# A list scheduler's keys, its model of a shared port, and the order of late loads in a single-core block kernel

## The chip, the cores and the metric

The kernel runs on one core of one Trainium2 chip. The metric is the device time of one execution in microseconds (us), taken as the median of several runs. Five instruction streams work beside each other: TensorE (PE; its weight loads, PEld, overlap its matmuls), VectorE (DVE), ScalarE (ACT), GpSimd (POOL) and SyncE (SP), which here only issues DMAs. Each stream runs its own list in order; between streams there are semaphores.

## The reference

One transformer block on 512 positions of width 1024, in float32: a hybrid attention (8 heads of "NSA": compressed, selected and window keys, gated; 8 heads of a sliding window of 128 with sinks), its output projection, a feed-forward part with a causal convolution (inner width 2816), and a gate from per-layer inputs.

```python
h = rmsnorm(x, attn_pre_g)
q_n, kc, vc, ksl, vsl, kwn, vwn, g_n, q_s, k_s, v_s = split(h @ w_in)
k_cmp, v_cmp = compress_kv(kc), compress_kv(vc)      # gelu(blocks @ w1) @ w2
o_nsa = nsa_attention(q_n, k_cmp, v_cmp, ksl, vsl, kwn, vwn, sigmoid(g_n))
o_swa = swa_attention(q_s, k_s, v_s, sinks)
x = x + rmsnorm(concat([o_nsa, o_swa]) @ w_o, attn_post_g)
a, u = split(rmsnorm(x, mlp_pre_g) @ w_gate_up)
y = (gelu(causal_dwconv(a)) * u) @ w_down
x = x + rmsnorm(y, mlp_post_g)
x = x + (p @ w_ple) * sigmoid(x @ w_ple_gate)
```

## The kernel before

**Arithmetic.** Each float32 operand of a product is split into a high part (a copy in TensorE's rounded format fp32r, mostly made by ACT) and a low part (operand minus high part, a "low pass", one two-operand pass of DVE or POOL). A product is three matmuls: high by high, low by high, high by low. Activations lie with features on the 128 partitions and the 512 positions along the free axis.

**Stages.** `load_x` (L632) loads x in eight chunks together with the weights wv, makes their parts and the sums of squares for the first norm. `v_natural` (L676) makes all values and the gates; `compress_in` (L744), `proj_k`, `proj_q` and `compress_out` (L814) make compressed keys and values, keys and queries. The first heads' scores start near 75 us. The attention runs over 16 units (a group of four heads by a block of 128 queries); between its steps PE gets "fill" products: the remaining key and query projections and the first part of the output projection. `out_proj` finishes the projection, adds up mo (the mixed rows) on DVE, sums their squares with `square_acc` (L558), and issues the loads of p, wple (the "e" product), the residual x and the first gate-up weights gu0 to gu3. Then comes the handover: `norm_add` (L1221) with the reciprocal root of the sums (`rstd_col`, L528: product r_pst on PE, r_rv on DVE, r2c on POOL), the eight products of `ple_tile` around it, and the MLP (mlpup, mlpdown) and the gate behind.

**What sets the order.** From `load_x` to the end of `out_proj` nothing is emitted directly. `Recorder` (L216) keeps each instruction as a `Node` (L165) with the nodes it depends on; tiles get their buffers only when the order is fixed. `schedule` (L280) is a list scheduler: it holds a clock for each stream, a duration for each instruction (`cost`, L245, times MARGIN), 0.2 us or so of lag between engines, the buffers and PSUM banks that are free, and a rate of the DMA wire. At each step it takes the engine whose next instruction could start first, and on it, of those that could start then, the one with the least key. The key is the earliest number, in written order, among the instruction and those that follow from it. `play` (L373) emits the result. The trace shows all these instructions under one line, L376 (L419 in the changed file). What is written behind `out_proj` keeps its written order, and shows as L197.

**Names.** In the trace a row reads output<-input by tile names: `loadx_u` the parts of x, `vnatural_pss` the banks of `v_natural`, `compress_psmm` that of compress's first product, `projk_wh` the parts of the key weights, `nsa_pss` scores, `nsa_nmp`/`nsa_nnm` maxima and sums of a softmax, `fill_wh` weights of fill products, `swa_u` 545 and 548 and `outproj_wr` 652 and 655 the raw gu0 to gu3, `outproj_wh` 649 to 657 their low parts, `outproj_s_605` the sum of squares.

Of the kernel before, what the change touches and what calls it, by code (L numbers as in the profile page):

```python
# [17 lines left out]
P = 128  # L18
T = 512
D = 1024  # L20
KC = D // P
# [52 lines left out]
MARGIN = 1.06  # L74
# [90 lines left out]
class Node:  # L165
    ins = None

    def __init__(self, n, engine, name, a, k):
# [4 lines left out]
        self.writes = [x for m, x in named if m in ("out", "accum_out")] + ([] if "out" in k else views[:1])  # L173
        if "out" not in k and not isinstance(a[0], View):
            self.writes = [x for m, x in named if m == "accum_out"]
# [40 lines left out]
class Recorder:  # L216
    ENGINES = dict(tensor="PE", scalar="ACT", vector="DVE", gpsimd="POOL", sync="SP")

    def __init__(self, nc, pools):
        self.pools, self.nodes, self.on, self.over = pools, [], False, False  # L220
        for e in self.ENGINES:
            setattr(self, e, Engine(self, e, getattr(nc, e)))

    def add(self, engine, name, a, k):
# [15 lines left out]
        for t in node.tiles:  # L240
            t.left += 1
# [3 lines left out]
    def cost(node):  # L245
# [5 lines left out]
        if e == "PE":  # L251
# [4 lines left out]
            return max(.058, .008 + .00043 * n)  # L256
        if e == "ACT":
            t = (.07 if psum else .1) + .00083 * n
            return t + (.17 if "accum_out" in node.k else .02)
        if e == "DVE":  # L260
            if name == "tensor_tensor_reduce":
                return .09 + .00103 * n + (.06 if not isinstance(node.k.get("scalar"), float) and n < 288 else 0)
            if name in ("tensor_copy", "tensor_scalar") and not psum:
                return .07 + .0006 * n
            if name == "memset":
                return .06 + .0007 * n
            if o.shape[0] < P and n >= 256:
                return .2 + .00104 * n
            return .07 + .00106 * n + (.06 if name == "scalar_tensor_tensor" else 0)
        if e == "POOL":  # L270
            if name in ("tensor_tensor",):
                return 1.05
            if name in ("tensor_sub", "tensor_mul", "tensor_add"):
                return .12 + .0023 * n
            if name == "tensor_scalar":
                return .33 + .00085 * n
            return .1 + .0009 * n
        return .05

    def schedule(self, live, begin):  # L280

        nodes = self.nodes
        lag = dict(PE=.25, ACT=.2, DVE=.2, POOL=.25, SP=.1)
        clock = dict(begin)
        for x in nodes:
            x.wait = len(x.deps)
            for d in x.deps:
                d.after.append(x)
        keep = {id(v.tile) for v in live}
        order, spare, have = {}, {}, {}  # L290
        seen = set()
        for x in nodes:
            for t in x.tiles:
                if id(t) not in seen:
                    seen.add(id(t))
                    spare.setdefault(t.key, [-99.0] * t.bufs)
                    if t.tile is not None:
                        spare[t.key].pop()
                    else:
# [1777 lines left out]
```

## Time and profile before

| what | value |
|---|---|
| median of 3 runs | 650.56 us (648.75 to 651.54) |
| the profiled execution | 652.84 us |
| its span in the profile | 651.1 us |
| granted TensorE clock, mean of the span | 0.996 |
| DVE, ACT and POOL busy | 511.8, 396.9 and 165.6 us |
| DMA moved | 95.78 MB, 147 GB/s in the mean |

The span is the profiler's time from the first to the last instruction of one execution. "Busy" counts an engine's instructions, so a pipelined matmul that waits a little still counts as busy. An idle time is put down to the semaphore that came last.

The stages lie in the trace as follows: loads and values until 30 us, first projections until 75, attention until 236, handover until 256, gate-up until 470, then down projection and gate. The page's slices show the granted clock at full speed except in the slice that holds 244 to 260:

```
PE   8999999999999999999999999999999999999997
PEclk9999999999999998999999999999999999999999
```

### The profile page before, as it was taken

Reading aid. Unit: us, or ns where it says so; the run is one execution under the profiler, and the core shown is the slowest. Engines: PE = TensorE matmul, PEld = TensorE weight load, DVE = VectorE, ACT = ScalarE, POOL = GpSimd, SP = SyncE. Lnnn points to the kernel's source line nnn. Section 1 sums busy time; section 2 is a strip of 40 time slices with the busy share of each in tenths; the row PEclk is TensorE's granted clock in tenths of the full one; section 3 lists DMA queues with packets and bytes.
Section 4 is the critical chain, followed back from the end, with each engine's and each line's share of the span. In section 5 each row is a group of like instructions: output and inputs, shape, how many; then the busy total and the mean of one; then the engine's idle time right before and its main releaser. Section 6 shows DMA issues by size and latency. Waiting matters only on the chain.

```text
span 651.1 us, 11311 instructions
## 1 busy us (share of the span) xinstructions
PE 640.6 (98%) x4071; PEld 578.2 (89%) x4071; DVE 511.8 (79%) x1023; ACT 396.9 (61%) x759; POOL 165.6 (25%) x246
## 2 busy tenths in 40 slices
PE   8999999999999999999999999999999999999997
PEld 7978778788888887888999999999998999999986
DVE  7596468788866675799899898998999985756873
ACT  7535477888889655666576767677764443333351
POOL 1010368876858350120101010011100010201000
PEclk9999999999999998999999999999999999999999
DMA  8416643210341637277465756758854334367032
GB/s 300 167 68 175 183 113 98 50 33 17 82 146 66 244 127 290 98 229 176 114 163 178 178 164 144 206 159 240 206 149 145 117 112 123 115 251 262 5 114 81
DMA packets 45289, 95.78 MB, mean 147 GB/s; under 512 B 4401, under 2 KB 13745, under 8 KB 44977
## 3 DMA queue, kind: packets, MB, share of 16 engines
q1 hardware_dynamic: 40208, 84.49, 39.3%
q0 software_dynamic: 4880, 10.49, 9.4%
q8 instruction: 32, 0.52, 0.3%
q14 instruction: 25, 0.20, 0.1%
q10 hardware_dynamic: 144, 0.08, 0.1%
HBM read 81.41 MB, written 9.44 MB: 140 GB/s over the span
## 4 chain that ended last, share of the span: by engine, by line
PE 91%; DVE 4%; ACT 2%; DMA 1%; issue 1%; DVEq 0%; SPq 0%
PE mlpup_psmm L197 23%; PE fill_psmm L376 8%; PE mlpup_pss L197 8%; PE mlpdown_pst L197 6%; PE mlpup_pst L197 5%; PE mlpdown_pss L197 5%; PE mlpdown_psmm L197 4%; PE norm_pss L197 3%; PE nsa_pso L376 3%; PE projq_psmm L376 3%; PE nsa_pst L376 3%; PE nsa_pss L376 2%; PE vnatural_pss L376 2%; PE mlpup_pso L197 2%; PE projk_psmm L376 2%; PE swa_pso L376 1%
## 5 line engine op out<-in xcount | busy, mean ns | idle before, releaser
L197 PE MATMUL mlpup_psmm<-r_u,mlpup_wh 128*128 128x256 f32 (+1 forms) x612 | 79.5, 283 | 0.1
L197 PEld LDWEIGHTS mlpup_psmm<-r_u,mlpup_wh 128*128 128x128 f32 x612 | 76.1, 191 | 0.6 <-DVE mlpup_wh L197 0.4
L197 PE MATMUL mlpup_psmm<-mlpup_u,mlpup_wh 128*128 128x256 f32 (+1 forms) x474 | 69.4, 297 | 0.0
L197 PEld LDWEIGHTS mlpup_psmm<-mlpup_u,mlpup_wh 128*128 128x128 f32 x474 | 63.5, 190 | 2.6
L197 POOL DMA_DIRECT2D mlpup_u<-in_gs_dram x17 | 20.9, 1230 | 155.8 <-DMA mlpup_u<-in_gs_dram 41.2
L197 ACT ACTIVATE mlpup_wh<-mlpup_u 128x1024 fp32r<-128x1024 f32 x37 | 39.2, 1060 | 25.6 <-PE mlpup_psmm L197 21.5
L197 ACT ACTIVATE mlpdown_wh<-mlpdown_wr 128x1024 fp32r<-128x1024 f32 (+1 forms) x24 | 23.7, 988 | 40.3 <-PE mlpdown_pst L197 10.9
L197 DVE TENSOR_TENSOR mlpup_wh<-mlpup_u,mlpup_wh 128x1024 fp32r<-128x1024 f32 x37 | 45.2, 1220 | 1.5 <-ACT mlpup_wh L197 0.5
L376 PE MATMUL fill_psmm<-loadx_u,fill_wh 128*128 128x512 f32 x144 | 45.1, 403 | 0.0
L197 PE MATMUL mlpdown_pst<-mlpup_u,mlpdown_wh 128*128 128x512 f32 (+1 forms) x228 | 44.9, 340 | 0.0
L376 POOL TENSOR_SCALAR nsa_u<-nsa_u,nsa_nrc,gate 128x512 f32<-128x512 f32 (+3 forms) x64 | 38.5, 612 | 12.4 <-DVE nsa_nrc L376 10.1
L197 PEld LDWEIGHTS mlpdown_pst<-mlpup_u,mlpdown_wh 128*128 128x128 f32 x228 | 37.0, 189 | 4.9
L197 DVE TENSOR_TENSOR mlpdown_wh<-mlpdown_wr,mlpdown_wh 128x1024 fp32r<-128x1024 f32 (+1 forms) x24 | 27.2, 1135 | 17.7 <-ACT mlpdown_wh L197 17.6
L376 ACT ACTIVATE nsa_u<-nsa_u,nsa_nnm 128x512 f32<-128x512 f32 (+3 forms) x64 | 35.3, 555 | 5.9 <-DVE nsa_nnm L376 4.6
L197 DVE TENSOR_TENSOR mlpup_wh<-mlpup_wr,mlpup_wh 128x1024 fp32r<-128x1024 f32 (+1 forms) x23 | 27.9, 1212 | 11.8 <-ACT mlpup_wh L197 11.8
L197 POOL TENSOR_TENSOR mlpdown_s<-mlpdown_s,mlpdown_s 128x512 f32<-128x512 f32 x6 | 9.5, 1578 | 106.3 <-ACT mlpdown_s L197 106.1
L197 PE MATMUL mlpdown_pss<-mlpup_u,mlpdown_wh 128*128 128x256 f32 x246 | 35.8, 282 | 0.0
L376 POOL TENSOR_TENSOR fill_wh<-fill_wr,fill_wh 128x1024 fp32r<-128x1024 f32 (+2 forms) x13 | 24.5, 1889 | 33.9 <-DVE compress_u L376 22.2
L197 PEld LDWEIGHTS mlpdown_pss<-mlpup_u,mlpdown_wh 128*128 128x128 f32 x246 | 32.5, 191 | 0.3
L376 DVE TENSOR_TENSOR nsa_u<-nsa_pst,nsa_u 128x512 fp32r<-128x512 f32 (+1 forms) x43 | 28.6, 685 | 4.5 <-ACT nsa_u L376 4.0
L376 DVE CUSTOM_DVE_ANT_0 nsa_u<-nsa_pss,biastables_u 128x128 f32<-128x128 f32 (+4 forms) x64 | 27.3, 446 | 5.0 <-PE nsa_pss L376 2.8
L197 PE MATMUL mlpdown_psmm<-mlpup_u,mlpdown_wh 128*128 128x256 f32 (+1 forms) x180 | 31.1, 320 | 0.0
(342 smaller groups left out, 1669.1 us busy)
## 6 DMA issues: line engine op xcount, KB each, us to landing
mlpup_u<-in_gs_dram SPq DMA_DIRECT2D x34, 512.0 KB, 5.0
mlpup_u<-in_gs_dram POOLq DMA_DIRECT2D x17, 512.0 KB, 6.2
mlpup_wr<-in_gs_dram SPq DMA_DIRECT2D x17, 256.0 KB, 3.9
fill_wr<-in_win_dram SPq DMA_DIRECT2D x6, 512.0 KB, 3.7
fill_u<-fill_u SPq DMA_DIRECT2D x20, 128.0 KB, 2.4
mlpdown_wr<-in_down_dram SPq DMA_DIRECT2D x5, 512.0 KB, 3.7
loadx_u<-in_xT_dram SPq DMA_DIRECT2D x8, 256.0 KB, 5.1
compress_u<-projk_u SPq DMA_DIRECT2D x16, 128.0 KB, 2.4
```

Of the source, the lines that this page charges most:

```text
L197: return f(*map(real, a), **{m: real(x) for m, x in k.items()})
L376: hold(x.call(*map(real, x.a), **{m: real(v) for m, v in x.k.items()}))
```

## The change

Five things are changed.

1. **Keys.** Before, an instruction's key came from written order alone. Now `play` plans six times. After each plan `dues` walks back through it: PE's instructions get the times at which PE would run them without any gap, every other instruction the latest time at which it may start so that whoever follows (also through a buffer that it frees) is in time, and these become the keys of the next plan. What the later stages want is given as time after PE's last recorded instruction: the e product's parts at 0, the sums of squares at 1.2, its second weights at 2.5, mo and x at 4.0, gu at 7.0. The plan with the earliest end is emitted.
2. **A shared port.** In the plan POOL's instructions, and DVE's passes over operands that lie in SBUF (those in SHARED that read no PSUM), exclude each other.
3. **Written order in `load_x`.** There ACT and DVE keep the order as written.
4. **Numbers.** Some durations, MARGIN, and the DMA rate (300 GB/s for 240) change; buffers that come free are told apart.
5. **Two edits of the program.** All sums of squares of `out_proj` are added on DVE (before: on POOL, but for the last). The dummy Exp that makes ACT load its table reads gv, the output of the second Gelu, where it read a constant.

```diff
-MARGIN = 1.06
+MARGIN = 1.1
+PASSES = 6
+SHARED = ("tensor_sub", "tensor_add", "tensor_mul", "scalar_tensor_tensor", "tensor_copy")
...
+        if self.strict and node.engine in ("ACT", "DVE"):
+            if node.engine in self.before:
+                node.deps.add(self.before[node.engine])
+            self.before[node.engine] = node
...
+    def link(self):
...
+            x.port = x.engine == "POOL" or x.engine == "DVE" and x.name in SHARED and not any(v.tile.psum for v in x.reads)
+            x.key = x.n if x.engine != "SP" else min([y.n for y in x.after] or [x.n])
+
+    def dues(self, done, begin, live):
+
+        t = begin["PE"]
+        for x in done:
+            x.due = 1e9
+            if x.engine == "PE":
+                x.due, t = t, t + x.cost
+        wanted = {id(v.tile): t + d for v, d in live}
+        for x in reversed(done):
+            nexts = x.after + [y for o in x.tiles for y in o.heirs]
+            due = min([y.due - (0 if y.engine == x.engine != "SP" else DELAY[x.engine]) for y in nexts] + [wanted[id(v.tile)] for v in x.writes if id(v.tile) in wanted] + [t + 9.0])
+            if x.engine == "PE":
+                x.key = min(x.due, due - x.cost)
+            else:
+                x.due = x.key = due - (TRANSFER_US if x.engine == "SP" else x.cost)
...
-            x.key = min([x.n] + [y.n for y in x.after]) if x.engine != "SP" else min([y.n for y in x.after] or [x.n])
...
+            if x.port:
+                t = max(t, port)
+                if x.engine == "DVE":
+                    t = max(t, clock["POOL"])
...
-                wire = max(wire, t + 1.8) + size / 240e3
+                wire = max(wire, t + 1.8) + size / 300e3
...
+        for _ in range(PASSES):
+            done, end = self.schedule(live, begin)
+            if best is None or end < best[0]:
+                best = end, done
+            self.dues(done, begin, live)
...
-        self.rec.on = True
+        self.rec.on = self.rec.strict = True
...
-        self.hold(nc.scalar.activation(self.tiny([P, 1], "act"), self.ones, AF.Exp))
+        self.hold(nc.scalar.activation(self.tiny([P, 1], "act"), gv[:, 0, 0:1], AF.Exp))
...
-            self.square_acc(acc, m, c == 0, c == KC - 1)
+            self.square_acc(acc, m, c == 0, True)
...
+        live = [(t, 0.0) for t in (*ple[0], *ple[1][0])] + [(acc, 1.2), *((t, 2.5) for t in ple[1][1])]
+        live += [(t, 4.0) for t in (*self.mo, *self.x1, *ple[2])] + [(t, 7.0) for w in self.upw for t in w]
```

In `load_x` itself the first instructions on DVE were, before, the low part of x's first chunk, the cast of the first wv and its low pass; now the cast and the low pass come first, and ACT makes each chunk's square two chunks later than before.

**In the first projections**, DVE's list shows the last two changes of place around compress's eviction (`compress_s` from the bank `compress_psmm`) and the low pass of the key weights (`projk_wh`). Before, all four value blocks stood ahead of these rows, and two casts of bias tables between:

```order
L376 TENSOR_TENSOR compress_s_75_471<-compress_psmm_74_368,r1b_412 64x32x8 x4
L376 COPY compress_s_75_471<-cols_78 128x8x2
L376 CAST biastables_u_90_486<-biastables_s_89_451 128x512
L376 CAST biastables_u_90_486<-biastables_s_91_464 128x128
L376 TENSOR_TENSOR projk_wh_94_494<-projk_wr_92_358,projk_wh_93_426 128x1024
L376 TENSOR_TENSOR compress_u_77_506<-compress_s_75_471,compress_u_76_489 128x528
```

Now (the first row belongs to the first value block, `vnatural_u_62` is the second):

```order
L419 RECIPROCAL gate_419<-vnatural_ge_60_397 128x24
L419 TENSOR_TENSOR projk_wh_94_422<-projk_wr_92_355,projk_wh_93_408 128x1024
L419 CAST vnatural_u_62_436<-vnatural_s_61_416 128x6x64
L419 TENSOR_TENSOR vnatural_u_62_436<-vnatural_s_61_416,vnatural_u_62_436 128x6x64
L419 TENSOR_TENSOR compress_s_75_447<-compress_psmm_74_370,r1b_406 64x32x8 x4
L419 COPY compress_s_75_447<-cols_78 128x8x2
L419 TENSOR_TENSOR compress_wh_100_466<-vnatural_u_67_360,compress_wh_99_438 128x1024
L419 TENSOR_TENSOR compress_u_77_476<-compress_s_75_447,compress_u_76_469 128x528
```

The low pass moved behind the first value block, the eviction behind the second; the casts of the bias tables moved elsewhere.

**Ahead of the first scores**, DVE's list shows the low pass of projk's second tile (`projk_u_141`) and the first scores' passes (`nsa_pss_159`, `160`). Before:

```order
L376 TENSOR_TENSOR projk_s_140_776<-projk_psmm_139_727,r1b_412 128x512
L376 TENSOR_TENSOR projq_u_130_767<-projq_s_129_729,projq_u_130_767 128x512
L376 TENSOR_TENSOR fill_wh_166_787<-fill_wr_164_719,fill_wh_165_773 128x1024
L376 SCALAR_TENSOR_TENSOR projq_s_146_820<-projq_psmm_145_771,qscale_124,r1b_412 128x512
L376 ISA nsa_pc_157_828,nsa_nnm_153_827<-nsa_pss_159_815,biastables_u_90_486 128x32
L376 ISA nsa_nnm_153_827 128x1
L376 ISA nsa_u_158_833,nsa_nmp_154_832<-nsa_pss_159_815,biastables_u_90_486 128x224
L376 ISA nsa_nmp_154_832 128x1
L376 ISA nsa_u_158_833,nsa_nnm_153_827<-nsa_pss_160_818,biastables_u_90_486,nsa_nmp_154_832 128x288
L376 ISA nsa_nnm_153_827 128x1
L376 TENSOR_TENSOR projk_u_141_830<-projk_s_140_776,projk_u_141_830 128x512
```

Now:

```order
L419 TENSOR_TENSOR projq_u_130_740<-projq_s_129_725,projq_u_130_740 128x512
L419 TENSOR_TENSOR projk_s_140_777<-projk_psmm_139_723,r1b_406 128x512
L419 TENSOR_TENSOR projk_u_141_783<-projk_s_140_777,projk_u_141_783 128x512
L419 TENSOR_TENSOR fill_wh_166_807<-fill_wr_164_768,fill_wh_165_795 128x1024
L419 SCALAR_TENSOR_TENSOR projq_s_146_822<-projq_psmm_145_774,qscale_120,r1b_406 128x512
L419 ISA nsa_u_158_832,nsa_nmp_154_831<-nsa_pss_159_817,biastables_u_90_570 128x224
```

The low pass of projk moved from behind the first head's scores to directly behind its eviction. On ACT the load of the Exp table moved from behind a copy of projk to directly behind the second Gelu. On PE, 19 fill products stand among the first heads' scores, where 28 stood.

**At the handover**, DVE's list shows the additions to mo (`swa_u_466`) and to the sum of squares (`outproj_s_605`), the low passes of gu (`outproj_wh`) and the first row of the norm (`r2_rv`). Before:

```order
L376 TENSOR_TENSOR outproj_wh_649_2982<-swa_u_545_2866,outproj_wh_648_2966 128x1024
L376 TENSOR_TENSOR swa_u_466_2824<-swa_u_466_2824,outproj_psmm_644_2973 128x512
L376 TENSOR_TENSOR outproj_wh_651_2999<-swa_u_548_2871,outproj_wh_650_2991 128x1024
L376 TENSOR_TENSOR swa_u_466_2824<-swa_u_466_2824,outproj_pss_646_2988 128x512
L376 TENSOR_TENSOR outproj_wh_654_3007<-outproj_wr_652_2913,outproj_wh_653_3003 128x1024
L376 TENSOR_TENSOR outproj_s_605_2925<-outproj_s_605_2925,outproj_s_647_3009 128x512
L376 TENSOR_TENSOR outproj_wh_657_3014<-outproj_wr_655_2941,outproj_wh_656_3011 128x1024
L197 TENSOR_SCALAR r2_rv_662_3047<-r2_pst_661_3042 128x4
```

Now:

```order
L419 TENSOR_TENSOR swa_u_466_2815<-swa_u_466_2815,outproj_psmm_644_2969 128x512
L419 TENSOR_TENSOR outproj_s_605_2920<-outproj_s_605_2920,outproj_s_643_2982 128x512
L419 TENSOR_TENSOR swa_u_466_2815<-swa_u_466_2815,outproj_pss_646_2980 128x512
L419 TENSOR_TENSOR pletiles_wh_629_2996<-swa_u_537_2848,pletiles_wh_628_2932 128x1024
L419 TENSOR_TENSOR outproj_s_605_2920<-outproj_s_605_2920,outproj_s_645_2994 128x512
L419 TENSOR_TENSOR outproj_s_605_2920<-outproj_s_605_2920,outproj_s_647_2998 128x512
L419 TENSOR_TENSOR outproj_wh_649_3006<-swa_u_545_2876,outproj_wh_648_2989 128x1024
L419 TENSOR_TENSOR outproj_wh_651_3010<-swa_u_548_2881,outproj_wh_650_3000 128x1024
L419 TENSOR_TENSOR outproj_wh_654_3012<-outproj_wr_652_2885,outproj_wh_653_3004 128x1024
L419 TENSOR_TENSOR outproj_wh_657_3014<-outproj_wr_655_2939,outproj_wh_656_3008 128x1024
L201 TENSOR_SCALAR r2_rv_662_3047<-r2_pst_661_3042 128x4
```

The low passes of gu, before between the additions, now stand in one row behind the last of them and ahead of `r2_rv`. SP's list changed with them. Before, the first half of x (`swa_u_538`, `542`) was loaded ahead of the last nine loads of wo, and p and wple (`swa_u_534`, `535`, `537`) ahead of the last two; now these two (`outproj_wr_630` and `635`) come first and all eleven others in one row behind, here with the last but one of them:

```order
L419 DMA outproj_wr_630_2803<-in_wo_dram 128x512
L419 DMA outproj_wr_635_2835<-in_wo_dram 128x4x256
L419 DMA swa_u_535_2840<-in_wple_dram 128x1024
L419 DMA swa_u_534_2844<-in_pT_dram 128x1024
L419 DMA swa_u_537_2848<-in_wple_dram 128x1024
L419 DMA swa_u_538_2855<-in_xT_dram 128x1024
L419 DMA swa_u_542_2862<-in_xT_dram 128x1024
L419 DMA outproj_u_640_2866<-in_xT_dram 128x1024
L419 DMA outproj_u_641_2872<-in_xT_dram 128x1024
L419 DMA swa_u_545_2876<-in_gu_dram 128x1024
L419 DMA swa_u_548_2881<-in_gu_dram 128x1024
L419 DMA outproj_wr_652_2885<-in_gu_dram 128x1024
```

Behind the handover the order on PE, DVE, POOL and ACT is the same; on SP two stores of e stand ahead of two loads of mlpup.

More of the change, by code (lines that the diff above doesn't have):

```diff
@@ L71 @@
 LAGS = [(1, 2), (2, 2)]
-MARGIN = 1.06
+MARGIN = 1.1
+PASSES = 6
+SHARED = ("tensor_sub", "tensor_add", "tensor_mul", "scalar_tensor_tensor", "tensor_copy")
+TRANSFER_US = 4.5
+DELAY = dict(PE=.25, ACT=.2, DVE=.2, POOL=.25, SP=.1)
+PATIENCE = dict(PE=.0, ACT=.0, DVE=.0, POOL=.0, SP=.0)
 BEGIN = dict(PE=5.4, ACT=4.0, DVE=1.5, POOL=2.0, SP=0.8)
@@ L275, in cost @@
             if name == "tensor_scalar":
-                return .33 + .00085 * n
-            return .1 + .0009 * n
+                return (.33 if isinstance(node.a[3], View) else .24) + .00085 * n
+            if name == "affine_select":
+                return .1 + .0022 * n
+            return .12 + .0008 * n
         return .05
[L280 to L286, printed above, removed]
+    def link(self):
+        for x in self.nodes:
@@ L287, in schedule @@
             for d in x.deps:
                 d.after.append(x)
[L289 to L299, printed above, removed]
-                        order.setdefault(t.key, []).append(t)
@@ L303, in schedule @@
+    def schedule(self, live, begin):
+        nodes, clock = self.nodes, dict(begin)
+        keep = {id(v.tile) for v, _ in live}
+        order, spare = {}, {}
+        seen, held = set(), set()
         ready = {e: [] for e in clock}
         for x in nodes:
-            if x.wait == 0:
+            x.wait, x.end = len(x.deps), None
+            if not x.deps:
                 ready[x.engine].append(x)
-        done, wire, gaps, table = [], -99.0, [], AF.Exp
-        held = set()
+            for o in x.tiles:
+                if id(o) not in seen:
+                    seen.add(id(o))
+                    o.left, o.heirs = len({id(u) for u, _, _ in o.uses}), []
+                    spare.setdefault(o.key, [(-99.0, n, None) for n in range(o.bufs)])
+                    if o.tile is not None:
+                        spare[o.key].pop()
+                    else:
+                        order.setdefault(o.key, []).append(o)
+        done, wire, table, port, serial = [], -99.0, AF.Exp, -99.0, 99
@@ L359, in schedule @@
             x.begin = t
+            if x.engine == "DVE" and x.port:
+                port = x.end
             ready[x.engine].remove(x)
@@ L368, in schedule @@
                 if o.left == 0 and id(o) not in keep:
-                    spare.setdefault(o.key, []).append(max(u.end for u, _, _ in o.uses) + .2)
-        self.gaps, self.done = gaps, done
-        return done
+                    serial += 1
+                    spare.setdefault(o.key, []).append((max(u.end for u, _, _ in o.uses) + .2, serial, o))
+        late = {id(v.tile): d for v, d in live}
+        return done, max([clock["PE"]] + [x.end + DELAY[x.engine] - late[id(v.tile)] for x in done for v in x.writes if id(v.tile) in late])
     def play(self, live, begin, hold):
         self.on = False
-        for x in self.schedule(live, begin):
+        self.link()
+        best = None
+        for _ in range(PASSES):
[3 more added lines that the diff above has]
+            self.dues(done, begin, live)
+        for x in best[1]:
             hold(x.call(*map(real, x.a), **{m: real(v) for m, v in x.k.items()}))
```

53 lines of the change are left out of this document (27 added, 26 removed).

## The prediction

> **What bounds the kernel now.** The page's first part, the list of waits of TensorE (PE) and the busy time by stage come first; in the stages each engine has its busy time and, in brackets, its instructions.
>
> ```profile
> PE 640.6 (98%) x4071; PEld 578.2 (89%) x4071; DVE 511.8 (79%) x1023; ACT 396.9 (61%) x759; POOL 165.6 (25%) x246
> ...
> PE r_pst L197 <- DVE outproj_s L376: 1.0, 1, 1.0
> PE nsa_pss L376 <- DVE nsa_nmp L376: 0.7, 1, 0.7
> PE vnatural_pss L376 <- ACT loadx_u L376: 0.7, 1, 0.7
> PE projk_psmm L376 <- DVE projk_wh L376: 0.6, 1, 0.6
> ...
> 0.00:20.00 20.00, 17.82 (x72) 16.34 (x73) 14.95 (x30) 14.24 (x26) 3.03 (x28) 1.00 0.72 245
> ...
> 160.00:180.00 20.00, 20.00 (x124) 17.24 (x124) 17.26 (x64) 17.64 (x53) 17.30 (x37) 1.00 0.25 68
> ...
> 240.00:260.00 20.00, 18.98 (x80) 14.72 (x79) 13.13 (x18) 12.38 (x21) 4.20 (x3) 0.91 0.60 230
> ...
> 360.00:400.00 40.00, 40.00 (x336) 40.00 (x336) 36.54 (x49) 28.36 (x48) 3.65 (x3) 1.00 0.63 167
> ```
>
> PE is the bound, with 98% of the span. What this change can save is PE's waits ahead of the handover to the later stages, about 256 us; behind it the order on PE, DVE and POOL stays word for word, and the stage at 360 is full. A busy PE hides part of a wait, because a matmul's record is longer than the spacing to the next: where it counts I take start to start. There are four places.
>
> **The start.**
>
> ```profile
> 0.79 3.64 DMA cols<-in_cols_dram
> ...
> 1.51 4.21 PE L197 MATMUL x_psmm<-x_s 128*128 128x512 f32 x9 [1.51 <-DVE x_s L197]
> 6.39 3.40 PE L376 MATMUL vnatural_pss<-loadx_u,loadx_u 128*128 128x408 f32 x9 [0.67 <-ACT loadx_u L376]
> 12.89 1.83 PE L376 MATMUL vnatural_pss<-loadx_u,loadx_u 128*128 128x408 f32 x9
> ...
> 5.21 0.75 DVE L376 SCALAR_TENSOR_TENSOR loadx_u<-loadx_u,cols,loadx_u 128x512 fp32r<-128x512 f32 x1 [0.28 <-ACT loadx_u L376]
> 5.88 0.37 DVE L376 CAST loadx_u<-loadx_u 128x408 fp32r<-128x408 f32 x1
> ```
>
> The first product waits for the cast of wv, which stands behind the 0.75 us pass on DVE. In written order the cast comes first. Its load is issued half a microsecond after that of cols; with the same 3.64 us it lands at 4.9, the cast ends at 5.3, and the products follow the warm-up ones (which end at 5.72 with their drain) without a pause, at about 5.5 instead of 6.39: 0.9 us. Then the clock: nine products take 3.40 us cold and 1.83 us warm. If PE still turns warm at 10.6, the head start is used on cold products and about 0.7 remains. If an unbroken run turns warm as soon after 1.51 as the second run did after 6.39 (4.2 us), nearly all of them are warm, and the passes on DVE, about 2.0 us a chunk, cap the gain near 2.2. I take 1.3, between them and nearer to what was seen.
> The Trainium skill, "TensorE: Matmul & The Clock Gate", section "Part 1: The HAM clock gate", says that the clock doubles after one full busy window of about 3.4 us, in windows that run freely. By that rule an unbroken run from 1.51 is warm by 8.3 at the latest, this term would be an estimated 1.7 at least, and the sum 0.4 more; here the clock rose 4.2 us after the pause ended, which fits the rule and doesn't decide it.
>
> **The first projections (30 to 50).** PE's rows, then DVE's:
>
> ```profile
> 30.46 8.21 PE L376 MATMUL compress_psmm<-loadx_u,compress_wh 128*128 128x512 f32 x35
> 38.84 0.47 PE L376 MATMUL projk_psmm<-loadx_u,projk_wh 128*128 128x512 f32 x1 [0.17 <-DVE compress_s L376]
> 39.63 0.33 PE L376 MATMUL compress_pss<-compress_wh,compress_u 128*66 128x256 f32 x1 [0.33 <-ACT compress_u L376]
> 40.55 1.66 PE L376 MATMUL projk_psmm<-loadx_u,projk_wh 128*128 128x512 f32 x6 [0.59 <-DVE projk_wh L376]
> ...
> 36.23 2.46 DVE L376 TENSOR_TENSOR compress_s<-compress_psmm,r1b 64x256 f32<-64x256 f32 x4
> 39.28 1.22 DVE L376 TENSOR_TENSOR projk_wh<-projk_wr,projk_wh 128x1024 fp32r<-128x1024 f32 x1
> ```
>
> 35 products that start at 30.46 every 0.23 us leave PE free at 38.5; two products later it is 40.55, of which 0.35 is work: 1.7 us lost. DVE held both: the eviction of the bank and the low pass of projk_wh stood behind the work for the values. Now the low pass follows the first value block and the eviction the second; against before, two value blocks of four (about 1.2 us each: cast, difference, gate) and two casts leave its front, and the transposes ahead of r1b stand four products (0.9 us) earlier. So the eviction ends some 2 us ahead of PE's need, and the 1.7 goes. What is late next is DVE: its low passes for compress come out only about half a microsecond ahead of PE's need. I charge 0.2 and take 1.5 (bounds 0.5, if they come a pass of 1.22 late, and 2.0).
>
> **The first scores (75 to 92).**
>
> ```profile
> 76.70 2.10 DVE L376 TENSOR_TENSOR projk_u<-projk_s,projk_u 128x512 fp32r<-128x512 f32 x1
> ...
> 75.86 2.40 POOL L376 TENSOR_TENSOR fill_wh<-fill_wr,fill_wh 128x1024 fp32r<-128x1024 f32 x1 [9.23 <-ACT fill_wh L376]
> ...
> 79.37 0.50 PE L376 MATMUL nsa_pss<-compress_u,projq_u 128*128 128x288 f32 x2 [0.69 <-DVE nsa_nmp L376]
> 83.06 0.93 PE L376 MATMUL nsa_pss<-compress_u,projq_u 128*128 128x512 f32 x3 [0.42 <-DMA compress_u<-projk_u]
> 88.33 1.12 PE L376 MATMUL nsa_pss<-compress_u,projq_u 128*128 128x256 f32 x6 [0.35 <-DVE nsa_nnm L376]
> ```
>
> A pass that takes 0.7 elsewhere took 2.10 while POOL worked on two SBUF tiles: here the two engines exclude each other. Behind it the first scores came late (0.69), and the window keys that it makes, moved by DMA, later still (0.42). Now this pass stands directly behind projk_s, some 6 us earlier, before POOL's; both waits go, and so does the table load between them on ACT, made earlier. With what the records hide, start to start, the waits here come to 2.2 us. The new order puts fewer fill products between the scores (19 for 28), so DVE, with 1.8 us a head, sets the pace there; I charge 0.6 and take 1.6 (bounds -0.5, where it sets the pace for one head more, and 2.2).
>
> **The middle (92 to 220).** PE is full at 160, but so nearly are DVE, ACT and POOL, 17.3 to 17.6 of 20 us. PE's waits there come to about 1.2 us in all. The reordering is large and not followed row by row: -0.3, bounds +1.2 and -2.5.
>
> **The handover (236 to 256).** PE, then DVE, POOL and SP:
>
> ```profile
> 242.72 1.56 PE L197 MATMUL r_pss<-pletiles_u,pletiles_wh 128*128 128x512 f32 x6
> 245.29 1.02 PE L197 MATMUL r_pst<-ones,outproj_s 128*128 128x1 f32 x8 [1.01 <-DVE outproj_s L376]
> 246.18 2.85 PE L197 MATMUL r_psmm<-pletiles_u,pletiles_wh 128*128 128x512 f32 x6
> 248.82 1.95 PE L197 MATMUL r_pss<-pletiles_u,pletiles_wh 128*128 128x512 f32 x6
> 250.61 1.55 PE L197 MATMUL r_psmm<-pletiles_u,pletiles_wh 128*128 128x512 f32 x6
> 252.00 0.60 PE L197 MATMUL r_pst<-ident,r2c 128*128 128x128 f32 x4
> ...
> 255.29 0.73 PE L197 MATMUL mlpup_pss<-r_u,outproj_wh 128*128 128x512 f32 x2
> ...
> 242.22 0.67 DVE L376 TENSOR_TENSOR swa_u<-swa_u,outproj_pss 128x512 f32<-128x512 f32 x1
> 242.81 1.73 DVE L376 TENSOR_TENSOR outproj_wh<-outproj_wr,outproj_wh 128x1024 fp32r<-128x1024 f32 x1
> 245.07 1.21 DVE L376 TENSOR_TENSOR outproj_wh<-outproj_wr,outproj_wh 128x1024 fp32r<-128x1024 f32 x1
> ...
> 246.59 1.04 POOL L197 TENSOR_TENSOR r2c<-r_rv,mhalf 128x4 f32<-128x4 f32 x1 [3.13 <-DVE r_rv L197]
> ...
> 219.46 2.76 SPq L376 DMA_DIRECT2D outproj_wr<-in_wo_dram  x2
> ...
> outproj_wr<-in_wo_dram SPq DMA_DIRECT2D x1, 512.0 KB, 3.6
> ...
> 222.00:232.00 10.00, 10.00 (x45) 8.26 (x45) 6.35 (x8) 5.00 (x8) 0.41 (x1) 1.00 0.89 319
> ```
>
> PE could start r_pst at 244.1 (six products after 242.72) and starts at 245.29: 1.2 us. After this pause two groups run cold, 2.64 and 1.79 start to start instead of 1.39: 1.65 us. Together 2.85. DVE was late because the low passes for gu (1.73 each beside POOL's sums of squares, 1.21 without) stood between the additions. Now POOL has no sums here, and they stand last. From PE's last output product (240.1) DVE needs, by starts: the addition 0.6, pletiles_wh 1.15, two sums 0.6 each, 243.2, so r_pst starts at 244.1. Then four gu passes of 1.15, and behind them in DVE's queue r_rv: 247.8; r2c on POOL 1.04, done by 249.3. PE (0.89 for r_pst, three groups of 1.39) needs it at 249.15. The gain is 2.7.
> The loads decide whether it stands. The inputs p, wple, x and gu, before spread from 182 on, are now 11 transfers of 512 KB in one row behind the last wo load. That is issued near 221.8 and lands 3.6 us later; 11 more at 319 GB/s take 18.1, so the last gu lands at 243.5. ACT's copies for PE's banks stand behind its high pass: it may land until about 245. At a tenth less speed it lands at 245.5 and costs half a microsecond, and up to 1.65 if PE turns cold again. Bounds 0.5 and 2.85.
>
> **The sum.** 1.3 + 1.5 + 1.6 - 0.3 + 2.7 = 6.8 us. The profiled execution took 652.84 us, its span of 651.1 and 1.7 around it: 646.0 for the like of it. It stands 2.3 above the median of the runs, 650.56; I take the gain as the same there: **643.8**. The best ends add up to 10.5, 640.1.
>
> **Rivals.** (1) The waits move: DVE can't hold the pace in the two middle places and the loads run late, so that only the start and half of the handover are won, 1.3 + 1.4: 647.9. For it: DVE already runs near 17 of 20 us wherever scores are made. Against it: PE's need in these rows lies behind what DVE's new order gives. (2) All ends come out well, with a warm start: 640 to 641. (3) Slower: POOL becomes the bound of the middle. It has 17.30 of 20 us at 160, and each of 16 units waits for its scaled rows. If holding the port back makes them late by 0.65 us a unit, PE loses 10.4, more than is won: 654. That decides from 0.42 a unit on (6.8 by 16). Against it: PE was full there with POOL as busy. (4) That it doesn't do what it says is out: the order has moved in the places above.
>
> **How the numbers follow.** The forecast, 641.5 to 647.2, has 0.58, rival 1 0.20, rival 2 0.10, rival 3 0.12. A measurement of this kernel tells about 0.5% (3.25 us) from no change; so faster 0.68, same 0.20, slower 0.12. From 640.0 to 650.0 only rival 3 and half of the extremes are left out.
>
> **What would show it.** Right: vnatural starts by 5.6; projk starts with compress's last product; no 2 us pass of projk_u; r_pst waits for nothing and the clock at 240 to 260 is 1.00. Wrong: PE waits for DVE passes at 45 to 52, for POOL's rows in the middle, or for DMA of pT, wple or gu after 225; or a group of products of 2.6 us, a cold clock, at a new place.

## The result, and the profile after

The changed kernel takes **641.1 us** (median of 4 runs, 640.89 to 641.29); before took 650.36 beside it (648.75 to 651.54). The ratio is 0.9859, with a 95% interval from 0.9837 to 0.9881. The profiled execution took 641.23 us, its span is 639.5 and its mean granted clock 0.999. The forecast was 643.8 (640.0 to 650.0): faster, inside the range, and 2.7 us too little.

The page's first part and PE's list of waits answer to those of before:

```profile
PE 633.3 (99%) x4071; PEld 575.6 (90%) x4071; DVE 511.1 (80%) x1029; ACT 396.3 (62%) x759; POOL 155.1 (24%) x240
```

```profile
PE x_psmm L201 <- DVE x_s L201: 1.5, 1, 1.5
PE vnatural_pss L419 <- DVE loadx_u L419: 0.3, 1, 0.3
```

Behind the start PE's list of waits is empty. The busy time by stage (start:end, length, then PE, PEld, DVE, ACT, POOL with instructions in brackets, granted clock, DMA share, GB/s) shows the same:

```profile
20.00:40.00 20.00, 20.00 (x101) 17.40 (x100) 15.01 (x27) 8.34 (x14) 1.58 (x2) 1.00 0.50 184
...
60.00:80.00 20.00, 20.00 (x101) 16.96 (x100) 12.10 (x55) 10.53 (x22) 7.17 (x5) 1.00 0.88 236
80.00:100.00 20.00, 20.00 (x117) 17.29 (x116) 14.25 (x58) 16.16 (x46) 19.47 (x30) 1.00 0.41 108
...
240.00:260.00 20.00, 20.00 (x90) 15.91 (x89) 17.06 (x25) 16.35 (x29) 0.65 (x2) 1.00 0.74 283
```

PE is at 20.00 of 20, also where POOL is at 19.47, and the stage of the handover has a clock of 1.00 where it had 0.91.

**Place by place.** The start of the changed kernel, PE and then DVE:

```profile
6.04 2.33 PE L419 MATMUL vnatural_pss<-loadx_u,loadx_u 128*128 128x408 f32 x9 [0.31 <-DVE loadx_u L419]
...
5.52 0.37 DVE L419 CAST loadx_u<-loadx_u 128x408 fp32r<-128x408 f32 x1 [0.26 <-DMA loadx_u<-in_wv_dram]
```

The cast now waits for its load and for nothing else. In this execution the load came at 5.49 (4.81 before), so the products start only 0.35 us earlier, at 6.04, and the prediction's sign "vnatural starts by 5.6" is not met in this profile; yet the nine take 2.33 us for 3.40, because the clock rises almost 4 us earlier (at 6.9 for 10.6). The first projections:

```profile
27.61 9.12 PE L419 MATMUL compress_psmm<-loadx_u,compress_wh 128*128 128x512 f32 x39
36.56 0.39 PE L419 MATMUL projk_psmm<-loadx_u,projk_wh 128*128 128x512 f32 x1
36.79 0.28 PE L419 MATMUL compress_pss<-compress_wh,compress_u 128*66 128x256 f32 x1
36.91 5.40 PE L419 MATMUL projk_psmm<-loadx_u,projk_wh 128*128 128x512 f32 x23
...
29.39 1.16 DVE L419 TENSOR_TENSOR projk_wh<-projk_wr,projk_wh 128x1024 fp32r<-128x1024 f32 x1
...
31.33 2.56 DVE L419 TENSOR_TENSOR compress_s<-compress_psmm,r1b 64x256 f32<-64x256 f32 x4
```

39 products from 27.61, projk right behind them at 36.56: the low pass is done at 30.6 and the eviction at 33.9, ahead of PE's need. Ahead of the first scores, DVE:

```profile
65.34 0.69 DVE L419 TENSOR_TENSOR projk_s<-projk_psmm,r1b 128x512 f32<-128x512 f32 x1 [3.85 <-PE projk_psmm L419]
67.28 0.69 DVE L419 TENSOR_TENSOR projk_u<-projk_s,projk_u 128x512 fp32r<-128x512 f32 x1 [1.24 <-ACT projk_u L419]
```

The pass that took 2.10 takes 0.69, and ends 2.6 us ahead of the first scores (70.58). The handover, PE, DVE and POOL:

```profile
234.13 1.55 PE L201 MATMUL r_pss<-pletiles_u,pletiles_wh 128*128 128x512 f32 x6
235.52 0.95 PE L201 MATMUL r_pst<-ones,outproj_s 128*128 128x1 f32 x8
236.32 1.66 PE L201 MATMUL r_psmm<-pletiles_u,pletiles_wh 128*128 128x512 f32 x6
...
240.61 0.60 PE L201 MATMUL r_pst<-ident,r2c 128*128 128x128 f32 x4
...
232.16 1.22 DVE L419 TENSOR_TENSOR pletiles_wh<-swa_u,pletiles_wh 128x1024 fp32r<-128x1024 f32 x1
233.29 1.48 DVE L419 TENSOR_TENSOR outproj_s<-outproj_s,outproj_s 128x512 f32<-128x512 f32 x2
234.69 2.35 DVE L419 TENSOR_TENSOR outproj_wh<-swa_u,outproj_wh 128x1024 fp32r<-128x1024 f32 x2
...
239.46 1.03 POOL L201 TENSOR_TENSOR r2c<-r_rv,mhalf 128x4 f32<-128x4 f32 x1 [25.65 <-DVE r_rv L201]
```

The last sum is done at 234.77, r_pst starts with the end of its six predecessors, and r2c is done at 240.49 for a need at 240.6.

**All runs in one table.** From the start of PE's first row of compress_psmm, nsa_pss, outproj_psmm and mlpup_pss in each profile: when compress starts, and how long the three stretches between take (us); then the profiled execution and the median of the runs. What follows takes 391.5 to 391.7 in all of them, up to the end of PE's last product. The profiled execution of `edits_alone` took 1267.44 us, about twice as long as the others, and is left out; its median is that of the other runs.

| run | compress | projections, to the first scores | first scores to output projection | handover, to gate-up | profiled | median |
|---|---|---|---|---|---|---|
| before | 27.02 | 47.72 | 148.88 | 31.67 | 652.84 | 650.36 |
| `before_again` | 27.09 | 47.69 | 148.17 | 31.67 | 652.11 | 651.61 |
| `before_warm11` | 25.11 | 47.71 | 148.16 | 30.09 | 648.60 | 650.16 |
| `squares_alone` | 25.29 | 47.72 | 148.24 | 29.14 | 647.88 | 649.47 |
| `strict_alone` | 24.53 | 47.60 | 147.89 | 30.12 | 647.64 | 648.31 |
| `port_alone` | 24.97 | 47.70 | 147.77 | 33.16 | 651.05 | 651.39 |
| `edits_alone` | | | | | | 646.67 |
| `plan_forced` | 24.22 | 45.46 | 146.79 | 33.21 | 646.97 | 647.20 |
| `neither` | 24.31 | 46.86 | 148.16 | 28.90 | 645.67 | 644.92 |
| `passes1` | 24.30 | 46.83 | 146.05 | 28.90 | 643.53 | 643.73 |
| `exp_undone` | 24.96 | 46.27 | 144.14 | 29.47 | 642.15 | 641.50 |
| `after_warm7` | 25.77 | 45.50 | 144.74 | 28.87 | 642.27 | 642.26 |
| `port_off` | 24.78 | 45.52 | 144.67 | 28.87 | 641.25 | 641.09 |
| changed | 25.11 | 45.47 | 144.45 | 28.87 | 641.23 | 641.10 |

Against the profiled execution of before that is 1.9 us at the start, 2.25 in the projections, 4.4 from the first scores to the output projection, 2.8 at the handover and 0.2 behind it: 11.6, 4.8 more than the sum of the prediction. Against the median it is 9.2. The two questions are where the 2.3 between them comes from, and where the 4.8.

### The profile page after: what moved, and what is told of

Its sections match the earlier page's. It is cut to its first block, busy times and chain, and to the rows that moved or that the text cites. A ratio compares the mean times of both kernels' runs of the same rounds, so it can differ in the third digit from the quotient of the medians.

```text
span 639.5 us, 11315 instructions
## 1 busy us (share of the span) xinstructions
PE 633.3 (99%) x4071; PEld 575.6 (90%) x4071; DVE 511.1 (80%) x1029; ACT 396.3 (62%) x759; POOL 155.1 (24%) x240
## 4 chain that ended last, share of the span: by engine, by line
PE 97%; ACT 1%; DMA 1%; DVE 0%; issue 0%; SPq 0%; ACTq 0%
PE mlpup_psmm L201 23%; PE fill_psmm L419 10%; PE mlpup_pss L201 8%; PE mlpdown_pst L201 6%; PE mlpdown_pss L201 5%; PE mlpup_pst L201 5%; PE mlpdown_psmm L201 4%; PE nsa_pss L419 3%; PE nsa_pst L419 3%; PE nsa_pso L419 3%; PE norm_pss L201 3%; PE projq_psmm L419 3%; PE mlpup_pso L201 2%; PE vnatural_pss L419 2%; PE projk_psmm L419 2%; PE compress_psmm L419 2%
## 5 line engine op out<-in xcount | busy, mean ns | idle before, releaser
L419 ACT ACTIVATE nsa_u<-nsa_pst 128x512 fp32r<-128x512 f32 x43 | 25.0, 596 | 12.0 <-PE nsa_pst L419 11.4
```

What stands on the lines that cost most here:

```text
L419: hold(x.call(*map(real, x.a), **{m: real(v) for m, v in x.k.items()}))
```

## The experiments

The theory: each place gained what its own wait had cost, by the order that the latest times give, and the start by PE's clock. The main rivals: the port in the plan did it, or the edits of the program alone, or the new durations.

### What before's runs differ by: `before_again`, `before_warm11`, `after_warm7`

> The kernel before, unchanged, profiled once more. Its profiled execution (652.84 us) lay 2.5 above the median of its runs, and its runs spread from 648.75 to 651.54, where those of the changed kernel spread over 0.4. Theory: TensorE's clock behind its two pauses (0.7 us at the start, 1.2 at the handover) is a lottery; behind each pause it either runs cold, at 1.6 us each, or not. Then the times fall near 652.8, 651.2 and 649.6, and the mean granted clock goes with them (0.996 in the long one, 0.998 or more in a short one). Rival: the loads arrive earlier or later; then the times spread without steps and the clock stays at 0.996.

Its profiled execution took 652.11 us, with a mean clock of 0.996. Together with the runs of before that stood beside the other experiments, 72 runs fall into groups: 11 from 648.5 to 649.0, all at a clock of 0.998 to 1.000; 37 from 650.0 to 650.9, all at 0.996 to 0.997; 18 from 651.5 to 652.4 at 0.996 to 0.997; and 6 from 651.0 to 652.0 at 0.999. The steps and the clock go as the theory says, though the sizes are not alike, 1.4 and 1.9. Four groups fit two pauses with two states each. The sum doesn't quite come out: a cold start with a full clock at the handover should lie near 650.8, and that group lies at 651.0 to 652.0; why is not shown.

> Before, with 11 warm-up products instead of 9 (they multiply zeros and nobody reads them), so that they end about when the first value product may start (6.4 us) and PE has no pause at the start. Runs of before fall into three groups, near 648.9, 650.3 and 652.2. Theory, that the pause of 0.7 us lets the start run cold in some executions: the group at 652.2 is gone, no run lies above 650.8, and the profiled one has a full clock by 8.5 us. Rival, that only the phase in which the clock's steps fall decides, pause or not: about a third of the runs stays near 652.

```diff
-WARM = 9
+WARM = 11
```

Ten runs: three from 648.6 to 649.0 (clock 0.998 to 0.999), seven from 650.1 to 650.3 (0.996 to 0.997), none above. PE's rows at the start of this kernel:

```profile
1.51 4.12 PE L197 MATMUL x_psmm<-x_s 128*128 128x512 f32 x11 [1.51 <-DVE x_s L197]
6.46 1.91 PE L376 MATMUL vnatural_pss<-loadx_u,loadx_u 128*128 128x408 f32 x9 [0.82 <-ACT loadx_u L376]
```

Eleven products in 4.12 us, where nine took 4.21: here the clock rose before they ended, so the pause didn't vanish (0.82), but it came too late to matter. The upper group is gone, as the theory said, but not by its means, since the pause is longer than before's 0.67. What the rival called the phase of the clock has its part: in `port_alone`, whose start is that of before, PE pauses for 0.60 us behind nine warm-up products as slow as before's, and its value products run at full pace from the first:

```profile
1.51 4.21 PE L197 MATMUL x_psmm<-x_s 128*128 128x512 f32 x9 [1.51 <-DVE x_s L197]
6.32 1.90 PE L387 MATMUL vnatural_pss<-loadx_u,loadx_u 128*128 128x408 f32 x9 [0.60 <-ACT loadx_u L387]
```

The step between the two groups that are left is the handover's, since 30.09 us there (profiled at 648.60) and 31.67 (in before) differ by 1.58 with the same wait for r_pst (1.0). Compress starts at 25.11, just as in the changed kernel.

> The changed kernel with 7 warm-up products instead of 9, so that they end 0.85 us earlier and PE pauses for 0.7 to 1.2 us ahead of the first value product, as long as before did or longer. Theory, that such a pause lets the start run cold in some executions and not in others: beside runs near 641.1 some lie near 642.8, and the spread over the runs grows from 0.4 to over 1.5 us. Rival, that the pause is nothing and the loads' arrival alone sets the start: all runs within 640.9 to 641.5.

```diff
-WARM = 9
+WARM = 7
```

Four runs: 640.58, and 642.25, 642.27, 642.60. The profiled one (642.27) is of the second kind:

```profile
5.43 3.40 PE L419 MATMUL vnatural_pss<-loadx_u,loadx_u 128*128 128x408 f32 x9 [0.57 <-DVE loadx_u L419]
```

With a pause of 0.57 us the nine products take 3.40 us again. With it three executions lie 1.7 us above the fourth, so the theory holds and its rival falls; with four runs this says little of how often. A pause leaves open whether the start runs cold, and does not decide it (`port_alone`).

### The edits one by one: `strict_alone`, `squares_alone`, `exp_undone`, `edits_alone`

> Before, with ACT and DVE in written order in load_x and nothing else changed. Theory, that the start's gain is the unbroken run of PE (a pause of 0.4 us or less keeps the clock rising): the first value product starts near 6.0, the clock is full by 7, compress's first product starts 1.9 us earlier than before (25.1 for 27.0), and since the later waits stay, the whole gains 1.5 to 2 us. Rival: the squares come later in written order, r1b is late, and DVE's queue gives the 1.9 back before 52; the whole is within 0.5 of before.

```diff
-        self.rec.on = True
+        self.rec.on = self.rec.strict = True
```

The first value product starts at 5.52, at the end of the last warm-up product, and compress at 24.53. Nothing of it is lost until 52 (47.60 us for the projections, 47.72 before). The ratio is 0.9968 (0.9950 to 0.9986), 648.31 us; four of the ten runs still have the clock of a cold handover (0.996 to 0.998). The 1.9 that the median gains (650.24 beside it) is the size that the theory gave, but not by the start alone: a cold handover came in four of these ten runs and in 19 of before's 25. Runs with the like clock lie 0.5 to 1.0 lower (near 647.9 for 648.9 with a full clock, near 649.7 for 650.2, before's commonest, without).

> Before, with the sums of squares of the output projection on DVE and nothing else changed. Theory of the prediction's handover, that POOL's sums beside DVE's low passes (1.73 us instead of 1.21) made r_pst late: r_pst waits for nothing, no product of its group runs cold, and from the last output product to the first gate-up product it takes 2.5 to 2.9 us less than before, about 647.7 in all. Rival, that the place of the low passes between the additions did it: DVE has six more additions of 0.6 us there, r_pst waits as long as before or longer, and the time is within 0.5 of before.

```diff
-            self.square_acc(acc, m, c == 0, c == KC - 1)
+            self.square_acc(acc, m, c == 0, True)
```

The handover of this kernel, PE and DVE, and PE's start:

```profile
240.34 1.56 PE L197 MATMUL r_pss<-pletiles_u,pletiles_wh 128*128 128x512 f32 x6
241.95 1.02 PE L197 MATMUL r_pst<-ones,outproj_s 128*128 128x1 f32 x8
242.83 1.64 PE L197 MATMUL r_psmm<-pletiles_u,pletiles_wh 128*128 128x512 f32 x6
...
239.19 1.22 DVE L376 TENSOR_TENSOR outproj_wh<-swa_u,outproj_wh 128x1024 fp32r<-128x1024 f32 x1
240.32 1.48 DVE L376 TENSOR_TENSOR outproj_s<-outproj_s,outproj_s 128x512 f32<-128x512 f32 x2
...
1.51 3.87 PE L197 MATMUL x_psmm<-x_s 128*128 128x512 f32 x9 [1.51 <-DVE x_s L197]
6.64 1.90 PE L376 MATMUL vnatural_pss<-loadx_u,loadx_u 128*128 128x408 f32 x9 [1.26 <-ACT loadx_u L376]
```

The low pass takes 1.22 us again, r_pst comes 0.2 us behind its predecessors (240.34 and six by 0.23), no group runs cold, and all ten runs have a clock of 0.999 to 1.000: 29.14 us for 31.67. So the old planner wins 2.5 of the handover's 2.8 with this one line, 1.6 of it by the clock. The line changed DVE's list too: before had three low passes ahead of the last sum, here two stand there and the third behind it. That the passes are shorter and that one has moved are not told apart, so the rival's cause, the place, may have its share. The median says less, 649.47 (ratio 0.9984, 0.9964 to 1.0003), since the start's two states stay: four runs lie near 647.8, where this start and this handover belong, three 1.7 to 1.9 higher, the step of a cold start, and three 2.7 to 4.4 higher, which no profile here explains.

> The changed kernel with the dummy Exp reading a constant, as before. Theory, that the load of ACT's table (1.28 us) comes back between the last copies of projk and the first scores and that PE waits for it: the first scores to the output projection take 0.4 to 1.3 us more than 144.5, 641.5 to 642.4 in all. Rival, that the plan with latest times finds room for it: within 0.3 of 641.1.

```diff
-        self.hold(nc.scalar.activation(self.tiny([P, 1], "act"), gv[:, 0, 0:1], AF.Exp))
+        self.hold(nc.scalar.activation(self.tiny([P, 1], "act"), self.ones, AF.Exp))
```

641.5, 0.4 more, but not where it was expected: the stretch behind the first scores is no longer (144.14); the projections take 0.8 more, with a wait of 0.5 for an eviction on ACT, and the handover 0.6 more. The edit is worth about 0.4 as part of this plan; that PE would wait for the table at the first scores is not shown.

> Before's planner, untouched, with the three edits of the program: written order in load_x, all sums of squares of the output projection on DVE, the dummy Exp behind the second Gelu. Theory, that each part of the gain sits where its edit is: first projections 47.6 us and first scores to output projection 147.9 (as with the written order alone), handover 29.1 (as with the sums alone), 646 to 647.2 in all, and no group of slow runs from a cold handover. Rival, that the edits interact with the old keys (DVE has six more passes ahead of its low passes): one of these stretches is over 0.7 longer, 648 or more.

The diff is the three above on the old planner. 646.67 us (0.9946, 0.9929 to 0.9964), inside the range that was the sum of the single edits' stretches. This is 3.5 of the 9.2, without any new key. Where its parts sit is not shown, for want of a profile at the usual speed.

### The planner: `passes1`, `port_alone`, `port_off`, `neither`, `plan_forced`

> The changed kernel with one planning pass: keys by written order, the port model, new durations, the two program edits and the strict start stay. Theory, that the latest times move what PE waits for: the start and the handover keep their gains (4.7 of 11.4 us), the waits of the first projections (2.2) and of the first scores and the middle (4.4) come back in large part, 644.5 to 647.5. Rival, that the port model and the durations do it: within 0.5 of 641.1.

```diff
-PASSES = 6
+PASSES = 1
```

643.73: less comes back than the theory said, more than its rival allowed. The projections lose 1.36 and the stretch behind them 1.6, which is one wait; PE, DVE and ACT of this kernel:

```profile
75.81 0.97 PE L419 MATMUL nsa_pss<-compress_u,projq_u 128*128 128x512 f32 x4 [1.89 <-DMA compress_u<-projk_u]
...
70.97 0.69 DVE L419 TENSOR_TENSOR projk_u<-projk_s,projk_u 128x512 fp32r<-128x512 f32 x1 [2.61 <-ACT projk_u L419]
...
70.31 0.63 ACT L419 ACTIVATE projk_u<-projk_s 128x512 fp32r<-128x512 f32 x1 [3.45 <-DMA projq_u<-projq_u]
```

The copy of projk waits 3.45 us for a buffer that the moves of projq still read; then low pass and moves are late, and PE waits 1.89 for the window keys. In the changed kernel the same low pass starts 3.7 us earlier. This is what the latest times mend here, not the pass's length.

> Before, with the shared port in the plan (POOL and DVE's two-operand passes over SBUF exclude each other) and nothing else changed. From the first scores to the output projection before takes 148.9 us, the changed kernel with one planning pass 146.1, the changed kernel 144.5. Theory, that the port in the plan is what the one-pass plan has over before: 146 to 147 us there, no pass of 2 us on projk_u. Rival, that the new durations and the written order did it: 148.5 to 149.5, within 0.5 of before as a whole.

```diff
+            if x.port:
+                t = max(t, port)
+                if x.engine == "DVE":
+                    t = max(t, clock["POOL"])
```

Neither side's numbers come out: the stretch takes 147.77, between the two ranges, and the whole 651.39 (1.0023, 0.9999 to 1.0047), 0.9 above before beside it; four of the ten runs take 654.6 to 655.4, with a clock of 0.994. At the first scores the theory holds. The pass of projk now stands behind POOL's and behind three heads' passes, and is short; up to 90 us PE's pauses of over 0.1 us come to 0.5 start to start, where before has 2.3 up to 92, and the wait of 0.69 for nsa_nmp is gone. What is won there is mostly lost to a new wait near 160, and the handover is worse. DVE's pass, and PE's list of waits:

```profile
76.80 0.69 DVE L387 TENSOR_TENSOR projk_u<-projk_s,projk_u 128x512 fp32r<-128x512 f32 x1
...
PE r_pst L197 <- DVE outproj_s L387: 2.5, 1, 2.5
...
PE nsa_pss L387 <- DVE nsa_nnm L387: 1.0, 1, 1.0
```

The plan doesn't hold on the chip either: at the handover two of DVE's low passes still take 2.13 and 1.72 us beside POOL's sums.

> The changed kernel, its plan without the shared port, everything else as changed (latest times, durations, both program edits, written order in load_x). Theory, that the port in the plan keeps DVE and POOL apart: passes of 1.7 to 2.1 us return on DVE and PE waits again between the first scores and the output projection, 145.5 to 147.5 us for 144.5 there, 642 to 644 in all. Rival, that the latest times alone put DVE's passes early enough: within 0.4 of 641.1.

```diff
-            x.port = x.engine == "POOL" or x.engine == "DVE" and ...
+            x.port = False
```

641.09 us, and every stretch within 0.25 of the changed kernel's. With latest times the port in the plan is worth nothing that can be measured here.

> The changed kernel with one planning pass and without the shared port in the plan: the fourth of four (both 641.1, latest times without the port 641.1, port without latest times 643.7). The durations, the written order in load_x and the two program edits stay. Theory, that port and latest times can stand in for each other in the first scores and the middle: without both the waits there come back, 148 us or more from the first scores to the output projection (144.5, 144.7 and 146.1 in the three others), 646 or more in all, like the three edits on the old planner (646.7). Rival, that the new durations did it: 146 to 147 there, 643.5 to 645 in all.

The diff is that of `port_off` and `passes1` together. The stretch is 148.16 long, as the theory said, but for another reason. PE's rows behind the same wait for the window keys, and the stage:

```profile
76.46 0.93 PE L419 MATMUL nsa_pss<-compress_u,projq_u 128*128 128x512 f32 x4 [1.92 <-DMA compress_u<-projk_u]
...
78.26 1.06 PE L419 MATMUL fill_psmm<-loadx_u,fill_wh 128*128 128x512 f32 x2
```

```profile
60.00:80.00 20.00, 17.73 (x79) 14.23 (x77) 9.60 (x34) 8.18 (x16) 5.99 (x3) 0.94 0.77 206
```

Behind the pause the clock falls: two products take 1.06 us for 0.63. From 77.5 to 80.9 the slow products cost 1.6 of the 148.16; two of the four runs don't have this cold stretch (clock 1.000; 642.59 and 644.17, for 645.67 and 646.10). The other 0.5 over `passes1` (146.05) is a wait for DVE's nsa_nmp at the first scores, which `passes1`, with the port in its plan, doesn't have. Behind 82 us PE never pauses for over 0.1 us until the handover, though neither port nor latest times are there. So the theory falls for the middle, and its rival, the new durations, stands: with what else the new planner's reckoning changed (the margin, the wire's rate, buffers told apart), for these weren't tried alone.

> The changed planner with the three edits of the program undone, and the last of its six plans emitted (with the sums on POOL none of the later plans ends earlier by its own reckoning than the first, which has keys by written order, so the choice of the best would emit that one). Theory, that the latest times own the projections and the middle whatever the edits: first projections 45.2 to 46.2 us, first scores to output projection 144 to 145.5, while the handover loses, since all low passes and POOL's sums stand ahead of r_pst: 32 to 36 for 28.9, 645 to 648 in all. Rival, that the middle needs the edits too: 147 or more there, 649 or more in all.

```diff
-            if best is None or end < best[0]:
-                best = end, done
+            best = end, done
```

The other hunks undo the three edits. The projections come out as the theory says (45.46), the handover too (33.21), the whole as well (647.2). The middle is between the two theories, 146.79: from 164 to 178 us there are eight pauses of 0.12 to 0.57 us. Why this plan has them and that of the changed kernel has not is open. PE's list of waits shows the price of the sums on POOL:

```profile
PE r_pst L201 <- DVE outproj_s L418: 2.4, 1, 2.4
```

## Why the prediction was right, and where it was not

**The start** (1.3 predicted, 1.9 against the profile, nothing against the median). The mechanism is right: the cast waits for its load alone, and where wv comes at 4.8, as in `strict_alone`, the products start at 5.52 (about 5.5 was said). In the changed kernel's own profile wv came only at 5.49, in `passes1` and `port_off`, with the same start, at 4.9; so that lateness is one execution's. The size is the clock's. The working saw that it hangs on the pause, and took one number; the runs have two states. By the rule of the Trainium skill, "TensorE: Matmul & The Clock Gate", section "Part 1: The HAM clock gate", that the clock doubles after a full busy window of about 3.4 us, an unbroken run from 1.51 would be at full pace by an estimated 8.3 at the latest. The traces of the starts without a pause agree: their products reach full pace between 5.8 (`plan_forced`) and 7.4 us (`exp_undone`), in `strict_alone` at 6.5 and in `port_off` at 6.9.

**The first projections** (1.5; 2.25, and the upper bound was 2.0). The step that failed is the stretch: PE's pauses were read to 40.6 and the waits behind, which the list put down to compress_wh and which cost 0.36 start to start, weren't in the sum; nor was the 0.2 for late low passes due. What did it is mostly the keys: 1.36 goes with latest times (46.83 to 45.47), 0.9 with the rest.

**The first scores and the middle** (1.6 and -0.3; 4.4). This is the step that failed most. Counted start to start, before has 15 pauses of over 0.1 us from the first scores to the output projection, 4.0 us together; the changed kernel has one, of 0.3. Up to 92 us they sum to 2.3, and 0.4 of shorter ones went with them, so that the first scores had no debit at all: the 0.6 charged for DVE setting the pace was not there. Behind 92 it was 1.4 and 0.4 of shorter ones. The prediction had 1.2 of waits there from the list, called a large reordering not followed row by row, and charged -0.3 for it; a plan that names no new wait deserved the list's 1.2. Of the 4.4 one repeat of before takes 0.7 back (148.17 for 148.88), a wait of 0.4 for the window keys that this run doesn't have.
The cause given for the first scores, that POOL and DVE exclude each other, fits the pass (2.10 and 0.69 us) and before's wait: in `port_alone`, with that pass short and behind the heads' passes, the wait for nsa_nmp is gone; its length and its place changed together and are not told apart. But a short pass is not enough for an early one: in `passes1` it takes 0.69 and PE waits longer, for the buffer of its copy. And the port in the plan moves nothing that the latest times don't (`port_off`).

**The handover** (2.7; 2.80). Right in each step: r_pst waits for nothing, the clock stays full, r2c is done 0.1 us ahead of its need. The loads, which were to decide it, came in time (the last gu lands at 232.6, behind a last wo at 216.8: 11 transfers in 15.8 us, where 18.1 were reckoned). What carries it is the one line on the sums, 2.5 without any new plan; and with the sums on POOL and the rest as changed, the planner, which reckons without the chip, puts the end of its first plan at 236.5 us and those of the five later ones at 237.8 to 238.7, so that it emits the first, with keys by written order. So this edit is also what lets the latest times in.

**From the profile to the median.** "I take the gain as the same there" is the other step that failed, the other way. The profiled execution of before had both pauses at their dear end. The commonest run has the start of `before_warm11` and a cold handover; from it to the changed kernel it is 0 at the start, 2.25, 3.7 (from 148.17), 2.8, and 0.2 behind: 8.95, and 9.1 are measured from 650.25. So 2.7 too little is 4.8 too little in the terms and 2.3 too much at the end, with 0.2 for rounding and the runs. That the forecast came out as near as 2.7 is in part luck: the two errors point in opposite ways.

**The rivals.** That the waits move and half is lost: no. That all ends come out well, 640 to 641: nearly, by other sizes. That POOL becomes the bound: it reaches 19.47 of 20 us at 80 and PE waits for none of its rows.

## What to carry to other kernels

Where a kernel's runs spread in steps, find out which step the profiled execution stands on before a gain read from it is carried to the median; closing a pause of half a microsecond may be worth three times its length, or nothing. A planner's new rule should be tried against the plain edits that came with it: here three of them, six additions moved to the other engine and one written order kept above all, gave 3.5 of 9.2 us with the old plan, while the rule on the shared port, which mended the first scores under the old keys, gave nothing beside latest times. Medians of kernels whose runs fall into groups are compared group by group: of the 1.9 that the median gained by the written order in `load_x`, 0.5 to 1.0 was left between runs of the like clock. And a plan is judged by its own reckoning of the end: with one stage fixed at a late end, it can't see what its other keys would win.

## What the runs showed of the hardware

A pause of PE of 1.2 to 2.5 us behind work at full pace may be followed by a cold clock, and in these traces the cold stretch has about the same length: 246.7 to 249.7 in before (pause 1.2 us, start to start), 77.5 to 80.9 in `neither` (2.1), 241.4 to 244.8 in `plan_forced` (2.5); in before and `plan_forced` these are 7 and 8 products at 427 ns for 226. Whether it comes is not the pause's length alone: in `before_warm11` and `strict_alone` the same pause of 1.2 leaves the clock full, in `passes1` one of 2.1 does, and in `squares_alone` 1.26 us at the start do, behind warm-up products that had already reached full speed (3.87 us for 4.21). At the start a pause may also come to nothing behind products that were all slow (0.60 us in `port_alone`).

The granted clock of the profile doesn't show the cold start: it reads 1.00 from 0 to 20 us while nine products take 3.40 us for 1.83. There the spacing of the products is to be read. The cold stretches further on it shows (0.91, 0.94).
